# Attention of a hybrid encoder: another place for the softmax division, another rotation, another order of the last half-heads

## The chip, the cores and the metric

One core of a Trainium2 chip runs the whole layer as one program. Its engines are TensorE (PE in the profile: matmuls and transposes), VectorE (DVE), ScalarE (ACT), GpSimd (POOL) and SyncE (SP, which only issues DMAs). Each works through its own instructions in order and waits on semaphores for the others. The time is that of the device, in microseconds, from one launch of the program; the median of several runs counts.

## The reference

One layer of an encoder is applied to two groups of 512 tokens of 1024 channels, in float32. A normalised input goes through one wide projection; its columns feed a recurrent branch (mLSTM) and an attention branch, and two sets of sigmoid gates that merge them. The attention part, and what takes up its result:

```python
qa = (rmsnorm(c_q, g_q) @ w_uq).reshape(B, S, A_HEADS, A_NOPE + A_ROPE)
q_nope = qa[..., :A_NOPE]
q_rope = rope(qa[..., A_NOPE:], cos[:, None, :], sin[:, None, :])
kv = (rmsnorm(c_kv, g_kv) @ w_ukv).reshape(B, S, A_HEADS, A_NOPE + A_V)
k_nope, va = kv[..., :A_NOPE], kv[..., A_NOPE:]
k_rope = rope(k_r, cos, sin)
y_a = mla_attention(q_nope, q_rope, k_nope, k_rope, va) @ w_ao
g_m, g_a = jnp.split(jax.nn.sigmoid(gm), 2, axis=-1)
x = x + (g_m * y_m + g_a * y_a) @ w_out
```

There are 8 heads with 128 plain and 64 rotary channels and 128 value channels. `rope` turns pairs of the 64 rotary channels: with halves x1 and x2 it gives (x1 cos - x2 sin, x1 sin + x2 cos). The attention is a softmax over all 512 tokens. y_m is the recurrent branch's product with w_mo.

## The kernel before

**Tiling.** Activations lie with channels on the 128 partitions and the 512 tokens of a group along the free axis. Every float32 operand of a matmul is split in two parts that the matmul takes: `hi`, a rounding copy made by ACT, and `lo`, the remainder made by DVE (`lo_of`). Each product is three matmuls: hi hi, lo hi, hi lo. So nearly every piece of data costs an ACT cast (0.6 us) and a DVE subtraction (0.7 us).

**Stages around the change.** First the merge gates, 16 pieces taken from the list `bulk` one by one by `merge_gate`, which PE does without waiting; then the first head's projections (`rot_proj`, `proj_hi`, `proj_lo`), the values of all heads (`v_proj`, L723 to L725), the attention loop, and the output products. PE begins the loop at about 640 us and the output products at 861.5.

**The attention loop** runs over 16 half-heads u (8 heads by 2 groups) in 17 rounds, as a pipeline: in round u the scores of u, the last transpose and the weighing of u - 1, and the projections of u + 1. `score` makes 128x512 scores in five matmuls and DVE their maximum (mx), `expo` the exponential with its row sum (ACT: p, den), `turn` and `turn_lo` four transposes (pt) and the split of their result (aph on ACT, apl on DVE), `weigh` the product with the values (av). The division comes after it: DVE takes the reciprocal of the four sums (rc), PE transposes them (`sums_row`), ACT copies them (rb), and two DMAs on POOL's queue write them to memory (rsd) and read them back as one row broadcast over 128 partitions (rb). In `weighed` ACT copies the product from PSUM (oz), POOL multiplies it by rb, and SP's queue writes it to memory (ozd). POOL also makes the remainder of the values (vl).

**Rotation.** `rope_steps` turns the rotary queries of two heads at once: four products with sin over 32 partitions (rs), one with cos, one sum over 128 partitions (rp). `rot_hi` and `rot_lo` then split them into the tiles qs, two casts and two subtractions of 64 partitions per group. This, the weights of later heads (`wa_hi`, `wa_lo`) and the first operands of the output products (`hop_hi` for P1, P2, P6 and P7) are spread over the rounds as filling.

**The output products** (`chain`) multiply by quads of weights in seven block products in place of eight (P1, P2, P7, P6, P5, Q4, P3); one quad is four 512x512 blocks of a weight pair. The operands are sums and differences of blocks: those of the activations are made in `Ops.part` (L913, L919, L920), those of the weights in `Seven.weights` (L972 to L982), on POOL or DVE. First come the four quads of the recurrent branch ("mo", operands hzd), then four of the attention ("ao", operands ozd).

**What sets the order.** In the loop `pinned` is set, and every engine keeps the order in which the code is written. Outside it, and for DMAs, a scheduler orders the instructions of each engine. DMA queues are SP's, ACT's (weights of the quads, `wst`) and POOL's. Tiles are taken from pools of slots; a new tile of a slot waits until its former one has been read.

Of the kernel before, what the change touches and what calls it, by code (L numbers as in the profile page):

```python
# [15 lines left out]
P = 128  # L16
# [46 lines left out]
def encoder_kernel(ctx: ExitStack, tc: tile.TileContext, a):  # L63
# [3 lines left out]
    class Engine:  # L67
# [5 lines left out]
        def __getattr__(self, name):  # L73
# [4 lines left out]
            def call(*args, **kw):  # L78
                r = f(*args, **kw)  # L79
                tc.keep_in_program_order(r)  # L80
                return r
# [619 lines left out]
    Q = Slots("Q", vt=2, rb=1, qkv=12, qst=4, p=3, ph=1, pl=1)  # L701
# [10 lines left out]

    def v_proj(half):
# [3 lines left out]
        for g in range(G):  # L717
            for i in range(NB):
                bk = bank()
# [6 lines left out]
                t = EV(("ch", "bk")[i % 2], "av")  # L726
# [10 lines left out]
    def rope_steps(t, s, nblk):  # L737
        n = 32 * nblk
        for i in range(nblk):
            f, o = slice(32 * i, 32 * i + 32), slice(32 * (i ^ 1), 32 * (i ^ 1) + 32)  # L740
            yield V.tensor_tensor(out=s[o], in0=t[f], in1=sin[f], op=ALU.mult)
        yield V.tensor_tensor(out=t[0:n], in0=t[0:n], in1=cos[0:n], op=ALU.mult)
        yield V.tensor_tensor(out=t[0:n], in0=t[0:n], in1=s[0:n], op=ALU.add)
# [24 lines left out]
    def rot_proj(m, g):  # L768
        t = rots[m, g] = AX("rt", "rp")
        S.copy(t, proj1(was[max(2 * m - 1, 0)], lat["cq"][g], 2, 0, "pj"))  # L770
        rsteps[m, g] = rope_steps(t, AX("rt", "rs"), 4)
# [5 lines left out]
    def rot_hi(m, g):  # L777
        t = rots[m, g]
        qst[m, g] = st = [Q("qst", "qs", F32R) for _ in range(2)]
        for i in range(2):  # L780
            f = slice(64 * i, 64 * i + 64)
            S.copy(st[i][f], t[f])

    def rot_lo(m, g):
        t, st = rots[m, g], qst[m, g]
        for i in range(2):
            f, o = slice(64 * i, 64 * i + 64), slice(64 - 64 * i, 128 - 64 * i)
            V.tensor_tensor(out=st[i][o], in0=t[f], in1=st[i][f].bitcast(F32), op=ALU.subtract)
# [17 lines left out]

    def score(u, i):
        hd, g = halves_[u]
        if i == 0:
# [3 lines left out]
                rc=sm.tile([P, NB], F32, name=nm("rc4"), tag="rc4", bufs=1),  # L813
# [11 lines left out]
    def expo(u, i):  # L825
# [4 lines left out]
        )  # L830

# [35 lines left out]
    def weighed(u):  # L867
# [81 lines left out]
    class Seven:  # L949
# [14 lines left out]
        def weights(self, name):  # L964
# [19 lines left out]
            return wsplit(src)  # L984
# [21 lines left out]
    def chain(quads, head=False, look=4):  # L1006
# [16 lines left out]
        made = {}  # L1023
# [49 lines left out]
    hops = Ops(hraw, None, lambda n: V if n == "P7" else GP)  # L1073
# [13 lines left out]
    def pair(kind, c, ops, put):  # L1087
        e = V if (kind, c) in (("mo", 3), ("ao", 0)) else GP
# [11 lines left out]
    for g in range(G):  # L1100
        rot(0, g, 6)
        rot_hi(0, g)
        rot_lo(0, g)
    kst = []
# [623 lines left out]
```

## Time and profile before

| | |
|---|---|
| median of 3 runs | 1901.38 us (1900.48 to 1904.08) |
| profiled execution, its own time | 1900.27 us |
| span of its instructions | 1898.3 us |
| mean granted TensorE clock | 0.989 |
| PE busy | 1841.2 us (97%) |
| DVE, ACT, POOL busy | 1241.7, 867.5, 420.2 us |

Rows of groups give busy time and the mean of one in ns, then idle time of the engine ahead of them and what ended it. Rows of waits give the waiting instruction and the one that released it, the total, the count and the longest. Rows of the time line give start and duration in us; times in brackets are idle time of the engine ahead of the row. In rows of stages each engine has its busy time in the stretch and its number of instructions; the last three figures are the granted clock of TensorE (1.00 is full speed), the busy share of the DMA engines, and GB/s. A row whose busy time overlaps the next is a pipelined one: matmuls of 0.39 us start every 0.23 us.

### The profile page before, as it was taken

To read this page: it belongs to the slowest core of one execution; us is meant where nothing else is said; L and a number is where in the kernel's file an instruction comes from. 1 tells how busy PE (TensorE), PEld (TensorE's weight loads), DVE (VectorE), ACT (ScalarE), POOL (GpSimd) and SP (SyncE) were. 2 spreads that over 40 slices of the span, in tenths; PEclk is the share of its full clock that TensorE was granted. 3 is DMA by queue.
4 is the path that set the end of the run, shared out by engine and by line. 5 is a ranking of instruction groups with operands and counts; after the bars stand their busy time and mean duration, and the time that the engine had idled before them with its cause. 6 is when DMAs were issued, how large, how long until landed. Compare 5 with 4: busy or idle time off the path is not lost.

```text
span 1898.3 us, 24423 instructions
## 1 busy us (share of the span) xinstructions
PE 1841.2 (97%) x8817; PEld 1526.5 (80%) x8817; DVE 1241.7 (65%) x2081; ACT 867.5 (46%) x1707; POOL 420.2 (22%) x328
## 2 busy tenths in 40 slices
PE   9999999999999999997999999999999999999997
PEld 7889898988887777775878888888888887878786
DVE  6758576766424688865798588445444569878756
ACT  6355556554222666663444356333333344434433
POOL 0100000100000123364031002666465523111000
PEclk9999999999999999998999999999999999999998
DMA  4211211112323423355564342232222347433332
GB/s 167 66 58 49 74 45 68 56 56 78 122 96 102 142 94 96 94 175 197 168 211 153 120 145 83 100 118 105 95 100 97 126 144 236 158 128 100 102 137 94
DMA packets 102024, 216.10 MB, mean 114 GB/s; under 512 B 11536, under 2 KB 22224, under 8 KB 101904
## 3 DMA queue, kind: packets, MB, share of 16 engines
q1 hardware_dynamic: 87456, 165.49, 25.6%
q10 hardware_dynamic: 12096, 43.00, 6.7%
q0 software_dynamic: 2352, 6.07, 1.0%
q8 instruction: 69, 1.13, 0.3%
q14 instruction: 51, 0.42, 0.1%
HBM read 160.24 MB, written 54.26 MB: 113 GB/s over the span
## 4 chain that ended last, share of the span: by engine, by line
PE 45%; DVE 5%; DMA 2%; issue 2%; POOL 1%; ACT 1%; ACTq 0%; SPq 0%; DVEq 0%; POOLq 0%
PE b L1001 12%; PE b L1003 12%; PE b L1002 12%; PE mm L79 2%; PE mm L185 1%; PE mm L184 1%; PE mm L183 1%; DVE xl L154 1%; PE mm L1521 1%; PE mm L1519 1%; PE mm L1520 1%; DVE wp L154 1%; DMA ld<-ozd 1%; POOL oz L79 0%; DMA rb<-rsd 0%
## 5 line engine op out<-in xcount | busy, mean ns | idle before, releaser
L1001 PE MATMUL b<-xh,wp 128*128 128x512 f32 x1148 | 441.7, 393 | 18.7 <-ACT wp L945 13.8
L1002 PE MATMUL b<-xl,wp 128*128 128x512 f32 x1148 | 447.6, 391 | 1.9 <-DVE xl L154 1.9
L1003 PE MATMUL b<-xh,wp 128*128 128x512 f32 x1148 | 444.8, 392 | 1.3 <-DVE wp L154 1.3
L945 ACT CAST wp<-wst 128x512 fp32r<-128x512 f32 (+1 forms) x270 | 164.3, 612 | 308.2 <-PE b L1003 254.4
L154 DVE TENSOR_TENSOR wp<-wst,wp 128x512 fp32r<-128x512 f32 (+1 forms) x270 | 230.2, 855 | 70.6 <-ACT wp L945 70.5
L1001 PEld LDWEIGHTS b<-xh,wp 128*128 128x128 f32 x1148 | 215.9, 188 | 71.7 <-ACT wp L945 17.2
L1002 PEld LDWEIGHTS b<-xl,wp 128*128 128x128 f32 x1148 | 216.0, 188 | 49.7 <-DVE xl L154 3.4
L1003 PEld LDWEIGHTS b<-xh,wp 128*128 128x128 f32 x1148 | 215.7, 188 | 49.4 <-DVE wp L154 2.7
L183 PE MATMUL mm<-hh,whi 128*128 128x512 f32 x560 | 219.5, 392 | 0.0
L184 PE MATMUL mm<-hl,whi 128*128 128x512 f32 x560 | 219.0, 391 | 0.0
L185 PE MATMUL mm<-hh,wlo 128*128 128x512 f32 x560 | 218.8, 391 | 0.0
L1047 DVE TENSOR_TENSOR u<-b,u 128x512 f32<-128x512 f32 x90 | 61.9, 688 | 133.8 <-PE b L1003 84.0
L185 PEld LDWEIGHTS mm<-hh,wlo 128*128 128x128 f32 x560 | 105.5, 188 | 22.2 <-DVE wlo L154 0.3
L184 PEld LDWEIGHTS mm<-hl,whi 128*128 128x128 f32 x560 | 105.6, 189 | 21.6
L183 PEld LDWEIGHTS mm<-hh,whi 128*128 128x128 f32 x560 | 105.6, 188 | 21.5 <-DVE to L382 0.2
L972 POOL TENSOR_TENSOR s<-wst,wst 128x512 f32<-128x512 f32 (+1 forms) x30 | 45.0, 1500 | 320.4 <-DMA wst<-wd 118.1
L168 ACT CAST whi<-wst 128x1024 fp32r<-128x1024 f32 x59 | 62.0, 1051 | 103.5 <-PE mm L184 64.4
L1418 POOL TENSOR_TENSOR sg<-sg,u 128x512 f32<-128x512 f32 x30 | 55.0, 1835 | 204.2 <-DVE u L1047 204.2
L1042 ACT COPY u<-b 128x512 f32<-128x512 f32 x90 | 50.7, 588 | 92.2 <-PE b L1003 66.9
L154 DVE TENSOR_TENSOR xl<-ld,xh 128x512 fp32r<-128x512 f32 x105 | 77.7, 769 | 15.2 <-ACT xh L929 14.6
L154 DVE TENSOR_TENSOR wlo<-wst,whi 128x1024 fp32r<-128x1024 f32 (+2 forms) x61 | 74.2, 1217 | 14.6 <-ACT whi L168 13.4
L79 POOL TENSOR_TENSOR vl<-avt,vh 128x512 fp32r<-128x512 f32 x16 | 20.7, 1291 | 282.3 <-ACT vh L79 282.3
(371 smaller groups left out, 3645.9 us busy)
## 6 DMA issues: line engine op xcount, KB each, us to landing
wst<-w SPq DMA_DIRECT2D x73, 512.0 KB, 3.3
wst<-w ACTq DMA_DIRECT2D x60, 512.0 KB, 3.6
ld<-actd SPq DMA_DIRECT2D x77, 256.0 KB, 2.8
actd<-t SPq DMA_DIRECT2D x40, 256.0 KB, 2.4
x<-x SPq DMA_DIRECT2D x32, 256.0 KB, 4.0
ld<-hzd SPq DMA_DIRECT2D x32, 256.0 KB, 3.5
wst<-wd ACTq DMA_DIRECT2D x16, 512.0 KB, 4.4
actd<-sg SPq DMA_DIRECT2D x30, 256.0 KB, 2.0
```

The costliest lines, as they stand in the source:

```text
L79: r = f(*args, **kw)
L154: e.tensor_tensor(out=out, in0=src, in1=hi.bitcast(F32), op=ALU.subtract)
L168: S.copy(hi[:, :n], st[:, :n])
L183: E.matmul(bk, whi[:, c], hi, start=k == 0, stop=False)
L184: E.matmul(bk, whi[:, c], lo, start=False, stop=False)
L185: last_mm[0] = E.matmul(bk, wlo[:, c], hi, start=False, stop=k == nk - 1)
L945: S.copy(hi, src)
L1001: E.matmul(bk, whi[:, c], hi, start=bool(first) and k == 0, stop=False, **sk)
L1002: E.matmul(bk, whi[:, c], lo, start=False, stop=False, **sk)
L1003: E.matmul(bk, wlo[:, c], hi, start=False, stop=k == self.kh - 1, **sk)
L1047: V.tensor_tensor(out=t, in0=b, in1=t, op=ALU.add if name == "P2" else ALU.subtract)
L1418: e.tensor_tensor(out=sg[at], in0=sg[at], in1=t, op=ALU.mult)
```

## The change

1. *Ahead of the loop*: 10 of the 16 merge gates stay where they were, 6 go between the projections and `v_proj`. The rotation of the shared key is done on 128 partitions and has moved ahead. `v_proj` takes its banks and its output tiles from other pools; the slot `vt` has one buffer in place of two.
2. *Rotation*: the rotary weights' columns are laid out so that the halves of two heads are 64 partitions apart. `rope_steps` needs two products with sin over 64 partitions, one with cos and one sum; the split is one cast and one subtraction over 128 partitions. `rot_put` then copies the 32-partition blocks into the tiles of two heads by eight DMAs on SP's queue.
3. *Division*: for u below 14 (`EVEN`), DVE multiplies the weighed values in PSUM by the broadcast reciprocals, late in the round; ACT's copy and POOL's product are gone. For u = 14 and 15, ACT scales each block of exponentials by its reciprocal ahead of the transposes (`inverse`, `even`), there is no broadcast, and ACT copies the weighed values out. All ozd writes are issued on POOL's queue.
4. *Filling*: the operands of the output products are made in the first and last of four rounds on DVE in place of POOL; the adds of the first mo quad's weights go to DVE. The weights of P1, P2 and P7 of that quad are split in rounds 13 and 14 (`ahead`).
5. *End of the loop*: the last round is written out by itself, with all its transposes behind the weighing of u = 14; `chain` is issued only after the last pinned instruction of DVE, ACT and POOL (`anchors`), with the two first quads already loaded.

```diff
-    Q = Slots("Q", vt=2, rb=1, qkv=12, qst=4, p=3, ph=1, pl=1)
+    Q = Slots("Q", vt=1, rb=1, qkv=12, qst=4, p=4, ph=1, pl=1)
...
-    def rope_steps(t, s, nblk):
-        n = 32 * nblk
-        for i in range(nblk):
-            f, o = slice(32 * i, 32 * i + 32), slice(32 * (i ^ 1), 32 * (i ^ 1) + 32)
+    def rope_steps(t, s):
+        for i in range(2):
+            f, o = slice(64 * i, 64 * i + 64), slice(64 - 64 * i, 128 - 64 * i)
             yield V.tensor_tensor(out=s[o], in0=t[f], in1=sin[f], op=ALU.mult)
...
+    def rot_put(m, g):
+        t, w = rots[m, g]
+        qst[m, g] = [Q("qst", "qs", F32R) for _ in range(2)]
+        for i, st in enumerate(qst[m, g]):
+            for b in range(4):
+                f = 32 * i + 64 * (b // 2)
+                nc.sync.dma_start(st.bitcast(F32)[32 * b : 32 * b + 32], (w, t)[b % 2][f : f + 32])
...
+    def inverse(u, i):
+        x = att[u]
+        V.reciprocal(out=x["rc"][:, i : i + 1], in_=x["den"][:, i : i + 1])
+
+    def even(u, i):
+        x = att[u]
+        S.activation(out=x["p"][i], in_=x["p"][i], func=AF.Copy, scale=x["rc"][:, i : i + 1])
...
         o = EV("ch", "oz")
-        S.copy(o, x["ob"])
-        GP.tensor_tensor(out=o, in0=o, in1=x["rb"], op=ALU.mult)
-        nc.sync.dma_start(ozd[g][hd], o)
+        if u >= EVEN:
+            S.copy(o, x["ob"])
+        else:
+            V.tensor_tensor(out=o, in0=x["ob"], in1=x["rb"], op=ALU.mult)
+        GP.dma_start(ozd[g][hd], o)
...
+        def ahead(self, name):
+            src = self.source(name)
+            t = wpair()
+            hi, lo = t[:, 0 : self.n], t[:, self.n : 2 * self.n]
+            self.w[name] = (hi, lo)
+            return (lambda: S.copy(hi, src)), (lambda: lo_of(lo, src, hi))
...
-    hops = Ops(hraw, None, lambda n: V if n == "P7" else GP)
+    hops = Ops(hraw, None, lambda n: V)
...
-        e = V if (kind, c) in (("mo", 3), ("ao", 0)) else GP
+        e = V if (kind, c) in (("mo", 0), ("mo", 3), ("ao", 0)) else GP
...
+    for _ in range(BULK[1]):
+        merge_gate(*bulk.pop(0))
...
+        if last:
+            score(u, 0)
+            expo(u, 0)
+            score(u, 1)
+            turn(u - 1, 3)
+            turn_lo(u - 1, 3)
+            expo(u, 1)
+            score(u, 2)
+            inverse(u, 0)
+            even(u, 0)
...
+            weigh(u - 1)
+            weighed(u - 1)
+            for i in range(NB - 1):
+                turn(u, i)
+                turn_lo(u, i)
+            continue
...
+    hops.r, hops.t, hops.sums = {}, {}, lambda n: GP
...
+    with ExitStack() as behind:
+        for i in anchors:
+            behind.enter_context(tc.issue_after(i))
+        quads += [pair("ao", c, oops, put_y(c)) for c in range(4)]
+        chain(quads, made=pairs)
...
-BULK = [16]
+BULK = [10, 6]
+EVEN = 14
```

DVE before, at the start of round 3: from the remainder of half-head 2's third block (apl) to half-head 2's reciprocal (rc); the maxima mx are half-head 3's, xl is filling, rs and qs are the rotation.

```order
L79 TENSOR_TENSOR apl_6538<-pt_6580,aph_6537 128x4x128
L79 TENSOR_TENSOR xl_6516<-ld_6201,xh_6515 128x512
L79 TENSOR_TENSOR rs_6458<-rp_6449,sin 32x512
L79 TENSOR_REDUCE mx_6592<-sc_6595 128x1
L79 TENSOR_REDUCE mx_6592<-sc_6608 128x1
L79 TENSOR_TENSOR qs_6602<-rp_6303,qs_6602 64x512
L79 TENSOR_TENSOR qs_6603<-rp_6303,qs_6603 64x512
L79 RECIPROCAL rc_996_6461<-den_6460 128x4
```

The same place of the changed kernel; oz is the division of half-head 1's output, ld a sum of the filling, rp the last step of the rotation.

```order
L79 TENSOR_TENSOR apl_6554<-pt_6597,aph_6553 128x4x128
L79 TENSOR_TENSOR oz_6606<-av_6534,rb_6528 128x512
L79 TENSOR_REDUCE mx_6619<-sc_6622 128x1
L79 TENSOR_TENSOR ld_6215<-ld_6215,ld_6211 128x512
L79 TENSOR_REDUCE mx_6619<-sc_6632 128x1
L79 TENSOR_TENSOR rp_6471<-rp_6471,rs_6472 128x512
L79 RECIPROCAL rc_1001_6483<-den_6482 128x4
```

Five operations stand there in place of six: the division has come in, two splits of the rotation and one product with sin have gone.

POOL before, at the end of the loop: the sums of the output products' operands (ld, L913, L919, L920; wst is a sum of weights) among the reciprocals' DMAs and the last products oz.

```order
L79 TENSOR_TENSOR oz_8205<-oz_8205,rb_8185 128x512
L913 TENSOR_TENSOR ld_8429<-ld_8429,ld_8431 128x512
L975 TENSOR_TENSOR wst_8545<-wst_8545,wst_8547 128x512
L913 TENSOR_TENSOR ld_8438<-ld_8438,ld_8440 128x512
L913 TENSOR_TENSOR ld_8447<-ld_8447,ld_8449 128x512
L913 TENSOR_TENSOR ld_8456<-ld_8456,ld_8458 128x512
L79 TENSOR_TENSOR vl_8297<-avt_8154,vh_8296 128x512
L79 DMA rsd_7_5884<-rb_8302 4x128
L919 TENSOR_TENSOR ld_8505<-ld_8505,ld_8429 128x512
L919 TENSOR_TENSOR ld_8515<-ld_8515,ld_8438 128x512
L919 TENSOR_TENSOR ld_8525<-ld_8525,ld_8447 128x512
L920 TENSOR_TENSOR ld_8505<-ld_8505,ld_8508 128x512
```

POOL now (L946, L952 and L953 are the former L913, L919 and L920; s is a sum of weights).

```order
L79 DMA ozd_6_5491<-oz_8317 128x512
L79 DMA ozd_7_5484<-oz_8396 128x512
L79 DMA ozd_7_5492<-oz_8442 128x512
L946 TENSOR_TENSOR ld_8468<-ld_8468,ld_8470 128x512
L946 TENSOR_TENSOR ld_8477<-ld_8477,ld_8479 128x512
L946 TENSOR_TENSOR ld_8486<-ld_8486,ld_8488 128x512
L946 TENSOR_TENSOR ld_8495<-ld_8495,ld_8497 128x512
L1005 TENSOR_TENSOR s_1556_8690<-wst_8052,wst_8054 128x512
L952 TENSOR_TENSOR ld_8535<-ld_8535,ld_8468 128x512
L952 TENSOR_TENSOR ld_8545<-ld_8545,ld_8477 128x512
L952 TENSOR_TENSOR ld_8555<-ld_8555,ld_8486 128x512
L952 TENSOR_TENSOR ld_8565<-ld_8565,ld_8495 128x512
```

The sums have moved behind the last output's write; five more of them (L1006 and four L953) follow.

ACT now, at the place where the first product of quad 2 gets its weights: xh are casts of POOL's sums, u copies of finished products, wp casts of weights.

```order
L978 CAST wp_8670<-wst_8050 128x512
L991 DMA wst_8729<-w 128x1024
L1085 COPY u_8591<-b_1498_8453 128x512
L978 CAST wp_8693<-s_1556_8690 128x512
L1085 COPY u_8609<-b_1538_8596 128x512
L978 CAST wp_8710<-wst_8048 128x512
L962 CAST xh_8541<-ld_8535 128x512
L991 DMA wst_8731<-w 128x1024
L962 CAST xh_8551<-ld_8545 128x512
L962 CAST xh_8561<-ld_8555 128x512
L1085 COPY u_8642<-b_1498_8453 128x512
L962 CAST xh_8571<-ld_8565 128x512
L978 CAST wp_8751<-wst_8729 128x512
```

The cast for quad 2 (wp_8751) stands behind four casts of sums that POOL makes last (xh_8541 to xh_8571); before, only the DMA of a later weight stood between (wst_8705), and the four casts stood earlier.

More of the change, by code (lines that the diff above doesn't have):

```diff
@@ L1133, in hop_hi, with hop_lo, ahead_hi, ahead_lo @@
         hlo[n] = (lo, src, hi)
+    def hop_lo(n):
+        lo_of(*hlo[n])
     hop_load(0)
+    v_load(0)
+    quads = [pair("mo", c, hops, put_z(c)) for c in range(4)]
+    ahead, anchors = {}, []
+    def ahead_hi(n):
+        hi, ahead[n] = pairs[0].ahead(n)
+        hi()
+    def ahead_lo(n):
+        ahead[n]()
     pinned[0] = True
     for u in range(NU + 1):
-        now, then, nxt = u < NU, u > 0, u + 1 < NU
+        now, then, nxt, last = u < NU, u > 0, u + 1 < NU, u == NU - 1
         m, r = u // 4, u % 4
@@ L1140, in encoder_kernel, with fill, p7_sum @@
         more = m < 3
-        def at(row, *alts):
-            return row == r and all(alts)
-        sub = None
-        if at(3, now):
-            hops.sums = lambda n: V if n == "P7" or m == 3 else GP
-            sub = hops.part("P6", m)
+        todo_ = {}
+        def fill(slot):
+            for f, *args in todo_.get(slot, ()):
+                f(*args)
+        if now and r == 0:
+            p7 = [None]
+            def p7_sum():
+                p7[0] = hops.part("P7", m)
+            todo_ = {
+                "a": [(p7_sum,)],
+                "mid": [(hop_hi, "P1", hops.part("P1", m)), (hop_hi, "P2", hops.part("P2", m))],
+                "d": [(hop_lo, "P1")],
+                "e": [(hop_lo, "P2")],
+                "late": [(lambda: hop_hi("P7", p7[0]),)],
+                "f": [(hop_lo, "P7")],
+            }
+            if more:
+                todo_["mid"].insert(0, (wa_hi, 2 * m + 1, RO))
+                todo_["d"].insert(0, (wa_lo, 2 * m + 1, RO))
+                todo_["end"] = [(rot_proj, m + 1, 0)]
+                if m == 0:
+                    todo_["late"].append((wa_hi, 1, QK))
+                    todo_["f"].append((wa_lo, 1, QK))
@@ new lines, in encoder_kernel, with p6_sum, p6_lo @@
+        if (more and r == 3) or (m == 3 and r == 1):
+            p6 = [None]
+            def p6_sum():
+                p6[0] = hops.part("P6", m)
+            def p6_lo():
+                hop_lo("P6")
+                if m < 3:
+                    hop_load(m + 1)
+            todo_ = {"a": [(p6_sum,)], "mid": [(lambda: hop_hi("P6", p6[0]),)], "d": [(p6_lo,)]}
+            if more:
+                todo_["b"] = [(rot_lo, m + 1, 1)]
+                todo_["late"] = [(wa_hi, 2 * m + 3, QK)]
+                todo_["f"] = [(wa_lo, 2 * m + 3, QK)]
+                todo_["end"] = [(rot_put, m + 1, 1)]
@@ L1179, in encoder_kernel @@
         if then:
[L1180 removed]
+            if u - 1 < EVEN:
+                V.reciprocal(out=att[u - 1]["rc"], in_=att[u - 1]["den"])
             turn_lo(u - 1, 3)
[L1182 to L1187 removed]
+        odd(u, 0)
+        fill("c")
         if nxt:
@@ L1259, in encoder_kernel @@
             WX = Slots("WX", "right", wst=2, s3=2, wp=1)
+            pairs = {i: quads[i][1]() for i in range(2)}
         if u == NU - 2:
```

229 lines of the change are left out of this document (104 added, 125 removed).

## The prediction

> **What bounds the kernel now.** I read the page's busy table, then the list of what TensorE waited for around the change, then busy time and clock by stage.
>
> ```profile
> PE 1841.2 (97%) x8817; PEld 1526.5 (80%) x8817; DVE 1241.7 (65%) x2081; ACT 867.5 (46%) x1707; POOL 420.2 (22%) x328
> PE b L1001 <- ACT wp L945: 11.4, 1, 11.4
> PE pt L79 <- DVE rc L79: 10.9, 9, 2.4
> PE mm L723 <- DVE ql L154: 2.9, 1, 2.9
> 653.00:840.00 187.00, 176.67 (x866) 140.10 (x865) 150.76 (x228) 123.03 (x275) 64.19 (x64) 0.99 0.32 98
> 840.00:862.00 22.00, 17.74 (x72) 13.09 (x71) 14.03 (x18) 8.79 (x21) 18.57 (x17) 0.84 0.63 223
> 862.00:900.00 38.00, 26.57 (x110) 21.42 (x109) 17.92 (x27) 13.28 (x26) 11.96 (x7) 0.87 0.62 214
> ```
>
> TensorE (PE) is busy 97% of the 1898.3 us span, and its matmuls stay what they are but for two transposes. So only PE's idle time, 57 us in all, and what runs at a lowered clock behind it can be won. Where the change reorders work, PE waits three times: 2.9 us ahead of the value projections, 10.9 us in nine pieces for the reciprocals of the softmax sums, 11.4 us at the boundary to the output products. Idle time is followed by a slow clock at some places and not at others (the last three figures are granted clock, DMA share and GB/s):
>
> ```profile
> 613.00:620.00 7.00, 6.41 (x19) 4.46 (x20) 6.40 (x11) 3.89 (x7) 0.00 (x0) 0.76 0.22 73
> 682.00:689.00 7.00, 6.69 (x27) 5.45 (x28) 4.46 (x7) 2.71 (x7) 2.35 (x3) 0.76 0.21 65
> 739.00:746.00 7.00, 7.00 (x36) 5.80 (x37) 5.79 (x8) 4.17 (x11) 2.37 (x3) 1.00 0.20 62
> 894.00:899.00 5.00, 4.03 (x11) 3.18 (x12) 3.69 (x6) 2.14 (x4) 0.00 (x0) 0.58 1.02 385
> ```
>
> Seven us at 0.76 lose 7 x 0.24 = 1.7 us; five at 0.58 lose 2.1 us. At 739 PE had paused about as long as at 682 and lost nothing. [...]
>
> **Ahead of attention.** Six merge gates now stand between the projections and the value projections: 288 matmuls at the 0.23 us of the rows at 861 (quoted below), 65 us of cover for the VectorE work that PE waited for. Gone are 2.9 us and the 1.7 of slow clock. I leave 0.7 for a wait between the two groups of value projections, which now share other buffers: **-3.9** (bounds -4.6, and 0 if the wait only moves).
>
> **The reciprocals.** In every half-head PE transposes the reciprocals, and waits when VectorE (DVE) reaches them late. Two places, DVE's rows and then PE's:
>
> ```profile
> 676.27 0.68 DVE L79 TENSOR_TENSOR apl<-pt,aph 128x512 fp32r<-128x512 f32 x1
> 676.87 0.68 DVE L79 TENSOR_TENSOR xl<-ld,xh 128x512 fp32r<-128x512 f32 x1
> 677.58 1.66 DVE L79 TENSOR_TENSOR rs<-rp,sin 32x512 f32<-32x512 f32 x1
> 679.26 1.29 DVE L79 TENSOR_REDUCE mx<-sc 128x1 f32<-128x512 f32 x2
> 680.58 1.39 DVE L79 TENSOR_TENSOR qs<-rp,qs 64x512 fp32r<-64x512 f32 x2
> 681.98 0.18 DVE L79 RECIPROCAL rc<-den 128x4 f32<-128x4 f32 x1
> 682.31 0.27 PE L79 MATMUL pt<-ident,rc 128*4 128x128 f32 x1 [2.42 <-DVE rc L79]
> 693.45 0.68 DVE L79 TENSOR_TENSOR wlo<-wst,whi 128x512 fp32r<-128x512 f32 x1
> 694.05 1.32 DVE L79 TENSOR_REDUCE mx<-sc 128x1 f32<-128x512 f32 x2
> 695.28 0.68 DVE L79 TENSOR_TENSOR rp<-rp,cos 128x512 f32<-128x512 f32 x1
> 695.88 0.69 DVE L79 TENSOR_TENSOR xl<-ld,xh 128x512 fp32r<-128x512 f32 x1
> 696.49 0.17 DVE L79 RECIPROCAL rc<-den 128x4 f32<-128x4 f32 x1
> 696.80 0.27 PE L79 MATMUL pt<-ident,rc 128*4 128x128 f32 x1 [0.33 <-DVE rc L79]
> ```
>
> From the end of apl (the remainder of the third block of softmax weights) to the reciprocal DVE works 5.1 us at the first place (676.87 to 681.98: six operations) and 3.0 us at the second (693.45 to 696.49: five). PE would have taken the result 5.1 - 2.4 = 2.7 us after that stretch began, and 3.0 - 0.3 = 2.7 at the second place: one constant. So the wait is the DVE work in that stretch less 2.7 us. In the new order the stretch holds, as the rows of the new order in the section on the change show for round 3, the division from PSUM, two maxima and up to two other operations: five in rounds 3, 4, 7, 8, 11, 12 and 13, at 0.6 each from start to start 3.1 us, a wait of 0.4; in the others less, or six behind a rotary projection that gives PE 1.4 us (six matmuls) more: none. The division reads PSUM like apl, whose 0.68 I take for it; bounds 0.6 to 1.7 (rs above, which stood against GpSimd). By this 7 x 0.4 = 2.8 us are left of 10.9 - 1.8 = 9.1 (the ninth piece, 1.8 us, is in the tail below): -6.3, and -1.7 of slow clock at 682. ScalarE (ACT) has a cast more in line in rounds 4, 8, 12 and 13: +0.5 in all. **-7.5** (bounds -8.5 and +1).
>
> The rest lies under PE outside these stretches. DVE had 150.8 of 187 us; 14 divisions at 0.68 add 9.5, five rotary operations per group in place of eight take away 18 at 0.6 or more, 11 us, and the sums that come over from GpSimd are a few at 0.68. If that cover failed, it would show as reciprocal waits, priced below. The rotated queries now go by eight small copies per group on SP's queue, 48 in the loop, with the value loads behind them, which have about half a half-head (7 us) to land.
>
> **The tail.** In the last two half-heads the division is done on ACT before the transposes.
>
> ```profile
> 845.13 0.27 PE L79 MATMUL pt<-ident,rc 128*4 128x128 f32 x1 [1.82 <-DVE rc L79]
> L79 ACT ACTIVATE p<-sc,mx 128x512 f32<-128x512 f32 x59 | 40.9, 693 | 24.1 <-DVE mx L79 24.0
> ```
>
> Two transposes (0.5) and the wait of 1.8 go; eight scalings come, of about 0.7 each by the exponential's 693 ns, the last of which stands between the last exponential and its transpose, with a reciprocal: 0.9 to 1.9, and the other three of that half-head partly. I put this at **0** (bounds -3 and +3).
>
> **The boundary.** Here is the chain of waits that led to PE's 11.43 us:
>
> ```profile
> 861.51 0.40 PE L1001 MATMUL b<-xh,wp 128*128 128x512 f32 x1
> 861.75 0.39 PE L1002 MATMUL b<-xl,wp 128*128 128x512 f32 x1
> 872.94 6.36 POOL oz L79
> 879.32 2.00 DMA ozd<-oz
> 881.82 5.50 DMA ld<-ozd
> 887.38 6.41 DMA ld<-ozd
> 893.87 0.33 ACTq L958
> 894.97 0.80 PE L1001 MATMUL b<-xh,wp 128*128 128x512 f32 x1 [11.43 <-ACT wp L945]
> ```
>
> GpSimd's (POOL) last product oz waits for the broadcast reciprocals and then runs 6.36 us; its write to memory (ozd) is next, SP's queue stands behind that, so its loads start late, and ACT's DMA for quad 2's weights goes only as the second of these lands. None of this is left: the last two half-heads' outputs are only copied by ACT, nothing waits for a broadcast there, and the ozd writes have left SP's queue for POOL's. 11.4 us and 2.1 of slow clock go.
>
> What is late next: the sums of the recurrent branch's halves. Before they ran beside the tail (POOL is busy 18.6 of the 22 us from 840 on); now they stand behind the last half-head on POOL, and ACT's casts of them stand ahead of its cast for quad 2's first product. PE starts the products at 861.5 and has eight before that one, 96 matmuls at 0.23: 22 us of cover. POOL needs 14 operations:
>
> ```profile
> L919 POOL TENSOR_TENSOR ld<-ld,ld 128x512 f32<-128x512 f32 x4 | 5.0, 1267 | 0.0
> 857.65 6.18 DVE L79 TENSOR_TENSOR xl<-ld,xh 128x512 fp32r<-128x512 f32 x1
> 872.64 1.89 DVE L154 TENSOR_TENSOR xl<-ld,xh 128x512 fp32r<-128x512 f32 x3
> 875.05 2.49 DVE L154 TENSOR_TENSOR xl<-ld,xh 128x512 fp32r<-128x512 f32 x4
> ```
>
> 14 x 1.27 = 17.8 us, from 1.5 us after PE's start (ACT's copy and two DMA issues come first), and two casts of 0.6: 20.5 us, so undisturbed they are just in time and PE waits 0. But DVE and POOL hold each other up: a DVE xl of 0.6 took 6.18 us under back-to-back sums at 857, and POOL's oz of 1.28 took 6.36 while DVE ran eight operations from 872.6 on. In the new stretch DVE has some 14 operations with two SBUF inputs, each waiting for a cast, so that they come singly. If each costs POOL half a microsecond (its own 0.6, not always in full), 7 us are added: 27.5 - 22 = 5.5 us of wait, and 1.6 of slow clock. If POOL's sums shut DVE out in a body, two spells of 6 us fall on the remainders that PE needs: 12, and 2.1. I take the alternating case: -13.5 + 7.1 = **-6.4** (bounds -13.5 and +0.6).
>
> [...]
>
> **Sum.** -3.9 - 7.5 + 0 - 6.4 = -17.8 us, from the profiled execution's own 1900.27: 1882.5. The runs' median is 1.1 above that execution, so I forecast **1883**.
>
> **Rivals.**
> - *The sums shut DVE out* (boundary +0.6 in place of -6.4): 1883 + 7 = **1890**. For it: the 6.18. Against: at 872 it was DVE that kept POOL out, and there it had the longer run of operations ready.
> - *No wait at the boundary*: 1883 - 7 = **1876**. For it: the 20.5 against 22. Against: it leaves 1.5 us for all contention.
> - *The reciprocal waits stay*, since the division was put into the very stretch that decides them: if one operation in the stretch doubles as rs did (1.66), each of 14 half-heads waits 1 us more or so, and the clock drops at one place or two: 7.5 + 1 less gain, **1891**. Against: the division has its input in PSUM, as apl has, whose 55 instances stay at 0.68.
> - *DVE waits for the broadcast.* The division now heads DVE's queue five operations before the reciprocal; behind it stand the maxima for which the exponentials and so PE's next transposes wait. The reciprocals' way through memory is POOL's:
>
> ```profile
> L79 POOL DMA_DIRECT2D rsd<-rb x15: 560/560/668, 656.1 to 852.2; - x15
> DMA to landing us min/median/max: 2.5/3.4/4.9
> ```
>
> From reciprocal to landing: 0.3 to PE, 0.3 transposes, 0.3 copy on ACT, 0.56 issue, 2.7 landing, 0.57, 3.4: 8.1 us. The next reciprocal comes 14.5 us after this one (681.98, 696.49), the division 3.1 before it: 11.4, so 3 us of margin, 1.5 with the longest landing. The outputs' writes of 256 KB now go on the same queue. If they hold the small ones up, DVE waits what exceeds 3 us, in 14 half-heads. To lose the whole gain and 3.8 us more it must be 21.6 / 14 = 1.5 us each, a landing 4.5 us later than now: **1905** or more. For it: a write takes 2.0 us (879.32) and nothing of that size was on this queue but the broadcast. Against: the write is issued after the broadcast has landed, and half a half-head ahead of the next small one.
>
> [...]
>
> **Chances.** Forecast 0.42; sums shut DVE out 0.16; no wait at the boundary 0.14; reciprocal waits stay 0.10; DVE waits for the broadcast 0.11; several of these costs at once, ending near the old time, 0.07. A measurement of this kernel tells about 0.2% (3.8 us) from no change. Faster: 0.42 + 0.16 + 0.14 + 0.08 of the fourth = 0.80; same: 0.07 + 0.02 = 0.09; slower: 0.11. The range runs from 1872 (no wait at the boundary, the tail 3 better, nothing left ahead of attention) to 1897 (sums shut DVE out, the tail 3 worse, half the reciprocal waits back) and leaves out the broadcast rival; the forecast's own is 1878 to 1888.
>
> **What would show it.** Right: no PE wait at the value projections; reciprocal waits of 3 us in all, in rounds 3, 4, 7, 8, 11, 12 and 13; no chain through ozd at the boundary, but one from POOL's sums over ACT's cast to the first product of quad 2, with 3 to 8 us of idle time; DVE's division near 0.68 us. Wrong: idle time of DVE ahead of the division (fifth case), of PE on value loads (SP's queue), or a division of 1 us and more. The stages behind 900 us keep their order on every engine, so they should last the same to 1 us; more would mean that something carries over.

## The result, and the profile after

The changed kernel takes 1883.89 us (median of 4 runs, 1881.14 to 1890.15), the one before 1902.73 us in the same rounds (1900.48 to 1905.74): a ratio of 0.9905 with a 95% interval of 0.9875 to 0.9934, some 19 us less. The profiled execution has a span of 1883.4 us. The forecast was 1883. That the total fits is luck: two terms of the sum missed, by about as much in opposite directions, as a table by stage shows. Its bounds are the same matmuls in both programs (their start times in the two traces).

| stage | before | changed | difference | forecast |
|---|---|---|---|---|
| matmul 2800 (at 499 us) to the first score | 140.99 | 137.65 | -3.3 | -3.9 |
| first score to the scores of half-head 14 | 188.93 | 181.59 | -7.3 | -7.5 |
| from there to the first output product | 33.77 | 34.64 | +0.9 | 0 |
| first to 192nd matmul of the output products | 57.03 | 56.21 | -0.8 | -6.4 |
| 192nd to 576th matmul | 92.82 | 93.47 | +0.6 | 0 |
| the rest | 886.96 | 880.49 | -6.5 | 0 |

What lies ahead of matmul 2800 is 1.6 us longer in this trace; over the kernels that follow it varies by 3.4 us, with the same instructions. With it the two traces lie 14.9 us apart, where the medians lie 19 apart: the changed kernel's traced execution took 1885.22 us, more than its median, and that of the kernel before 1900.27, less than its own. In the traced executions of two experiments (e7 and e9) the matmuls of the output products took 843 and 828 ns on average in place of 390 (spans of 5577 and 4728 us), with a recorded granted clock of 1.00. So PE's times cannot be read from these two, and what slowed PE there (throttling, says the expectation of e9) is not shown.

What TensorE (PE) waited for between 590 and 900 us, now (waiting instruction, releaser, us, times, longest):

```profile
PE b L1046 <- DVE wp L155: 10.9, 1, 10.9
PE pt L79 <- DVE rc L79: 4.3, 11, 1.0
PE pt L79 <- DVE apl L79: 3.0, 1, 3.0
PE mm L725 <- ACT wvh L159: 1.7, 1, 1.7
PE pt L79 <- ACT p L79: 1.4, 2, 0.7
PE av L79 <- ACT aph L79: 0.9, 2, 0.7
```

The waits for reciprocals went from 10.9 to 4.3 us, but at the boundary there is a wait of 10.9 us where there was one of 11.4. It is another wait. Here are VectorE (DVE), GpSimd (POOL) and PE in the time line at that place:

```profile
854.62 18.86 DVE L155 TENSOR_TENSOR wp<-wst,wp 128x512 fp32r<-128x512 f32 x2 [3.78 <-ACT wp L978]
855.03 5.04 POOL L946 TENSOR_TENSOR ld<-ld,ld 128x512 f32<-128x512 f32 x4
860.04 1.28 POOL L1005 TENSOR_TENSOR s<-wst,wst 128x512 f32<-128x512 f32 x1
861.29 4.93 POOL L952 TENSOR_TENSOR ld<-ld,ld 128x512 f32<-128x512 f32 x4
866.19 1.25 POOL L1006 TENSOR_TENSOR wst<-wst 128x512 f32<-128x512 f32 x1
867.41 4.91 POOL L953 TENSOR_TENSOR ld<-ld,ld 128x512 f32<-128x512 f32 x4
872.93 0.80 PE L1046 MATMUL b<-xh,wp 128*128 128x512 f32 x1 [10.87 <-DVE wp L155]
```

POOL's 14 sums follow each other from 855.03 to 872.3 without a gap, 17.3 us. In DVE's row two subtractions are merged. The first, the remainder of the weights for P6, the fourth product, has 0.7 us of work and lasts 18.26 us, to 872.87, half a microsecond after POOL has ended. The second, for the product behind it, takes 0.68. PE has only P1, P2 and P7 and two matmuls of P6 ahead of its wait, from 853.3 to 862.1.

In the loop, this is round 3 again, from the end of apl at 676.1:

```profile
676.12 0.68 DVE L79 TENSOR_TENSOR oz<-av,rb 128x512 f32<-128x512 f32 x1
676.72 0.68 DVE L79 TENSOR_REDUCE mx<-sc 128x1 f32<-128x512 f32 x1
677.31 0.68 DVE L79 TENSOR_TENSOR ld<-ld,ld 128x512 f32<-128x512 f32 x1
677.91 0.68 DVE L79 TENSOR_REDUCE mx<-sc 128x1 f32<-128x512 f32 x1
678.51 0.68 DVE L79 TENSOR_TENSOR rp<-rp,rs 128x512 fp32r<-128x512 f32 x1
679.11 0.17 DVE L79 RECIPROCAL rc<-den 128x4 f32<-128x4 f32 x1
679.43 0.27 PE L79 MATMUL pt<-ident,rc 128*4 128x128 f32 x1 [0.28 <-DVE rc L79]
```

Five operations, 3.0 us, no operation over 0.69: a wait of 0.28 where it was 2.42.

### The profile page after: what moved, and what is told of

Read it like the earlier page. It is cut to its first block, busy times and chain, and to the rows that moved or that the text cites. A ratio compares the mean times of both kernels' runs of the same rounds, so it can differ in the third digit from the quotient of the medians.

```text
span 1883.4 us, 24476 instructions
## 1 busy us (share of the span) xinstructions
PE 1831.4 (97%) x8815; PEld 1525.6 (81%) x8815; DVE 1238.8 (66%) x2084; ACT 860.7 (46%) x1690; POOL 393.3 (21%) x316
## 4 chain that ended last, share of the span: by engine, by line
PE 47%; DVE 7%; issue 1%; ACT 1%; DMA 0%; ACTq 0%; DVEq 0%; POOLq 0%
PE b L1044 12%; PE b L1046 12%; PE b L1045 12%; PE mm L79 2%; DVE wp L155 2%; DVE xl L155 1%; PE mm L186 1%; PE mm L184 1%; PE mm L185 1%; PE mm L1606 1%; PE mm L1607 1%; PE mm L1608 1%; ACT p L79 0%; DVE x L1543 0%; DVE t L943 0%
## 5 line engine op out<-in xcount | busy, mean ns | idle before, releaser
L155 DVE TENSOR_TENSOR wp<-wst,wp 128x512 fp32r<-128x512 f32 (+1 forms) x268 | 248.1, 928 | 68.9 <-ACT wp L978 68.7
L383 DVE TENSOR_TENSOR tg<-rs,mm 128x512 f32<-128x512 f32 x32 | 22.0, 686 | 82.8 <-PE mm L186 77.6
```

The source lines that it names most:

```text
L155: e.tensor_tensor(out=out, in0=src, in1=hi.bitcast(F32), op=ALU.subtract)
```

## The experiments

Each experiment changes the changed kernel by the diff shown and was timed in five rounds beside the kernel before on the same chip. Stage lengths are those of the table above; the changed kernel has 137.65, 181.6, 34.6, 56.2.

### e1: the changed kernel again

> The changed kernel itself, on the chip and in the rounds in which the next three run. Both theories: about 19 us less than the kernel before (1883 against 1902), with the 10.9 us wait of PE at the fourth product (P6, quad 0) again, and one VectorE weight remainder (wp) that lasts 18 to 19 us for two operations.

1884.75 us against 1904.53 (ratio 0.990, 0.9885 to 0.9915), a PE wait of 10.84 us at the same matmul, and stages of 137.65, 181.52, 34.34 and 56.30 us. The stages up to the 576th matmul repeat to 0.3 us, so they tell apart what the whole times do not. The tail repeats less well across kernels: it is 32.8 us in e8 and 33.6 in e2, whose edits do not touch it.

### e2: the boundary's sums on VectorE

```diff
-    hops.r, hops.t, hops.sums = {}, {}, lambda n: GP
+    hops.r, hops.t, hops.sums = {}, {}, lambda n: V
```

> The sums for P5 and Q4 (12 operations) at the boundary on VectorE in place of GpSimd, nothing else. Theory A (GpSimd's gapless run of 14 sums shuts out VectorE's weight remainder): GpSimd's run is 3 operations, no wp operation lasts over 3 us, and PE's wait at P6 falls from 10.9 to about 1 to 3 us, since VectorE now makes 12 sums at 0.6 (7 us) within the 8.2 us of cover that P1, P2 and P7 give; no slow clock after it. 8 to 11 us faster than the changed kernel. Theory B (the remainder waits for its cast, its weights or a buffer, and the sums only run at the same time): the wait stays or grows by the 7 us of added VectorE work; 0 to 7 us slower. Theory C (the operands for Q4 come late anyway): the wait moves to Q4 or to quad 2 and stays 8 us or more; no difference.

1878.37 us, ratio 0.9861 (0.9846 to 0.9875). PE's waits at the boundary are now these two:

```profile
PE b L1044 <- ACT wp L978: 1.5, 1, 1.5
PE b L1046 <- DVE wp L155: 1.0, 1, 1.0
```

The stage is 48.5 us, 7.7 shorter, though DVE has 7 us more to do in it. Behind the 1.5 us the clock was halved again (the stretch of 1.49 us in the last section). By the ratios the kernel is 7 to 8 us faster than the changed one, where 8 to 11 were expected. This is theory A; B and C would have kept the wait.

### e3: only the sums for Q4 on VectorE

```diff
-    hops.r, hops.t, hops.sums = {}, {}, lambda n: GP
+    hops.r, hops.t, hops.sums = {}, {}, lambda n: V if n == "Q4" else GP
```

> Only the 8 sums for Q4 on VectorE, the 4 for P5 left on GpSimd. Theory A: GpSimd's gapless run is 4 sums and 2 or 3 weight sums, 8 to 9 us from its start in place of 17.3, so the held remainder ends 8 to 9 us earlier than in the changed kernel and PE's wait falls from 10.9 to 2 to 3 us; 8 to 10 us faster than the changed kernel. Theory B: wait unchanged. Theory C: the wait moves to Q4 or quad 2.

1880.12 us, ratio 0.9877 (0.9861 to 0.9894): by the ratios 4 to 5 us less than the changed kernel, where 8 to 10 were expected. DVE, POOL and PE:

```profile
852.02 8.95 DVE L155 TENSOR_TENSOR wp<-wst,wp 128x512 fp32r<-128x512 f32 x2 [3.70 <-ACT wp L978]
852.44 5.04 POOL L946 TENSOR_TENSOR ld<-ld,ld 128x512 f32<-128x512 f32 x4
857.45 1.27 POOL L1005 TENSOR_TENSOR s<-wst,wst 128x512 f32<-128x512 f32 x1
869.34 0.50 PE L1046 MATMUL b<-xh,wp 128*128 128x512 f32 x1 [4.28 <-DVE wp L155]
```

Fewer sums, a shorter hold: the first of the two merged subtractions, P6's, lasts 7.25 us in place of 18.26 and ends at 859.27, again half a microsecond after the end of POOL's run (five sums, to 858.72). PE does not wait for it at all. The wait of 4.3 us is another one, two products later: it is for P5's remainder (868.61 to 869.29), which stands behind sums that DVE now makes. The stage is 49.9 us. So in these two traces the length of DVE's operation went with that of POOL's run: 18.26 us with 17.3, 7.25 with 6.3.

### e4: output products not held behind the loop

```diff
-        for i in anchors:
+        for i in anchors[:0]:
```

> The output products are no longer held behind the last instruction of the loop; GpSimd's sums run beside the last two half-heads. Theory A: most of GpSimd's run is over when the weight remainder comes, PE's wait at the boundary falls to 0 to 4 us, but VectorE's remainders of those sums and ACT's casts get into the tail: tail 0 to 6 us longer; in all 3 to 10 us faster than the changed kernel. Theory B: the boundary wait stays near 11 us.

1884.61 us, ratio 0.9898 (0.9883 to 0.9913): no difference. The boundary stage is 43.9 us with no wait, 12.3 shorter, but the tail is 49.9 us, 15.3 longer: the hold has moved there.

```profile
839.18 11.26 DVE L1015 TENSOR_TENSOR wst<-wst 128x512 f32<-128x512 f32 x1
852.30 2.07 PE L79 MATMUL av<-apl,vh 128*128 128x512 f32 x4 [8.31 <-DVE apl L79]
```

With nothing held back, a weight sum of the output products also got into DVE's queue ahead of the softmax remainders, was shut out for 11.26 us, and PE waited for what stood behind it. The hold again ended half a microsecond after POOL's run (849.89). Theory A had the boundary right, but gave the tail 0 to 6 us more.

### e5: the division behind the reciprocal

```diff
+        if 1 < u < NU:
+            weighed(u - 2)
...
             odd(u, 3)
-            if then:
-                weighed(u - 1)
```

(`weighed(u - 2)` stands just behind `turn_lo(u - 1, 3)`, and in the last round behind `even(u, 1)`.)

> VectorE's division (oz) is moved from five operations ahead of the next reciprocal to just behind it; nothing else. Theory D (PE's wait for the reciprocal is VectorE's work in that stretch less 2.7 us): the stretch is 0.6 us shorter in every round, the reciprocal waits fall from 4 us in 11 pieces to at most 0.7, and the loop is 3 us shorter. Theory E (the waits come from something else, such as the maxima or the accumulator read): waits unchanged, or moved to the weighing, which now waits for the division: 0 to 5 us longer.

1892.47 us, ratio 0.9953 (0.9939 to 0.9966), where the changed kernel had 0.990 to 0.9905: 9 to 10 us slower, and the loop is 191.64 us, 10 longer.

```profile
PE av L79 <- DVE oz L79: 12.2, 13, 1.6
PE pt L79 <- DVE rc L79: 1.4, 3, 0.8
```

The reciprocal waits fell in the sense of theory D, from 4.3 to 1.4 us (at most 0.7 was expected). But there is one bank for the weighed values: the next weighing now waits for the division, 13 times. A term that theory D left out decided. Theory E had named it, at 0 to 5 us. The division's place ahead of the reciprocal is the cheaper one.

### e6: the division on GpSimd again

```diff
-            V.tensor_tensor(out=o, in0=x["ob"], in1=x["rb"], op=ALU.mult)
+            S.copy(o, x["ob"])
+            GP.tensor_tensor(out=o, in0=o, in1=x["rb"], op=ALU.mult)
```

> The division of the first 14 half-heads again as before the change: copy from PSUM on ScalarE, product on GpSimd; all else as changed. Theory F (the division on VectorE does not by itself win the loop; the shorter rotation and the order do): reciprocal waits fall from 4 to about 1 us as in the late division, rotation steps rise to 0.8 or more beside GpSimd's products: loop from 2 us shorter to 1 longer. Theory G (taking GpSimd's products out of VectorE's way is what won): the reciprocal waits come back to 8 to 11 us and the loop is 4 to 8 us longer.

1883.98 us, ratio 0.9904 (0.9889 to 0.9919): the same as the changed kernel; the loop is 182.16 us, 0.6 longer. So moving the division to DVE is worth next to nothing by itself. Round 3, DVE and POOL:

```profile
674.85 1.59 DVE L79 TENSOR_TENSOR ld<-ld,ld 128x512 f32<-128x512 f32 x1
674.62 1.28 POOL L79 TENSOR_TENSOR oz<-oz,rb 128x512 f32<-128x512 f32 x1 [5.03 <-ACT oz L79]
PE pt L79 <- DVE rc L79: 4.1, 10, 0.8
```

DVE has one operation less in the stretch, but the sum beside POOL's product takes 1.59 us in place of 0.68: what is saved is lost to the hold. Theory F has the size; that the waits would fall to 1 us it had wrong.

### e7 and e9: the weights of P6 and of quad 1's P1 ahead of the sums

```diff
         else:
+            for q, n in ((0, "P6"), (1, "P1")):
+                hi, lo = pairs[q].ahead(n)
+                hi()
+                lo()
             weighed(u - 1)
```

> The remainders of the weights of P6 (quad 0) and P1 (quad 1) are made before the last half-head's output copy, so before GpSimd's sums begin; GpSimd's run of 14 stays. Theory A (lock): the next VectorE operation with two inputs from SBUF is held to the end of the same run instead, but PE has five products of cover in place of three, 5.5 us more: wait 10.8 to 5 us, 5 to 6 us faster than the changed kernel. Theory B (late cast, weights or buffer of that one remainder): no wait of more than 2 us is left, 9 us or more faster.

> The kernel of e7 once more, since e7's profiled execution had TensorE throttled throughout (span 5577 us) and shows nothing of the boundary; its other six executions had a median of 1883.96. Theory A (lock): the wait is less than 10.8 but not gone, 3 to 6 us, at the next remainder with two SBUF inputs, which ends with GpSimd's run of sums. Theory B: no wait over 2 us at the boundary.

Medians of 1884.29 and 1882.61 us, ratios 0.9908 (0.9893 to 0.9924) and 0.9884 (0.9869 to 0.9899): by the ratios between 1 us more and 4 us less than the changed kernel, where 5 to 6 less were expected. PE's wait cannot be read from these traces. What DVE and POOL did can; this is e9:

```profile
2129.93 17.07 DVE L155 TENSOR_TENSOR xl<-ld,xh 128x512 fp32r<-128x512 f32 x1 [7.09 <-ACT xh L962]
2127.96 4.96 POOL L946 TENSOR_TENSOR ld<-ld,ld 128x512 f32<-128x512 f32 x4
2145.19 1.26 POOL L1008 TENSOR_TENSOR wst<-wst,wst 128x512 f32<-128x512 f32 x1
```

The two remainders were done ahead, in 0.7 us each, and the next operation with two inputs from SBUF, an operand's remainder, was held 17.07 us, to the end of POOL's run. So the hold did not belong to that one remainder, its cast or its buffer: here it fell on the operation that came next. Why the time fell by less than the cover of two more products stays open.

### e8: the merge gates back

```diff
-BULK = [10, 6]
+BULK = [16, 0]
```

> All 16 merge gates ahead of the projections again, none between these and the value projections. If they were the cover: PE's wait ahead of the first value projection is back, 1 to 3 us (the rotation there is four VectorE products in place of eight, so less than the 2.9 of before is possible), with 1.7 us of slow clock if it is over 2.4; the 1.7 between the two groups stays: 1 to 4.5 us slower than the changed kernel. If the shorter rotation had already removed the wait: no difference within 0.5 us in the trace.

1884.37 us, ratio 0.9909 (0.9892 to 0.9925). The first stage is 136.45 us: 1.2 shorter than with the gates as cover, and PE waits for

```profile
PE mm L725 <- ACT wvh L159: 1.7, 1, 1.7
```

alone. Neither expectation had this. The gates were not what took the wait of 2.9 us away; between the projections they even cost a wait of 0.9 us at their start.

### e10: the rotation in pieces of 32 partitions

```diff
         for i in range(2):
-            f, o = slice(64 * i, 64 * i + 64), slice(64 - 64 * i, 128 - 64 * i)
-            yield V.tensor_tensor(out=s[o], in0=t[f], in1=sin[f], op=ALU.mult)
+            for j in range(2):
+                b = 64 * i + 32 * j
+                f, o = slice(b, b + 32), slice((b + 64) % 128, (b + 64) % 128 + 32)
+                q = V.tensor_tensor(out=s[o], in0=t[f], in1=sin[f], op=ALU.mult)
+            yield q
```

> Each product with sin is made in two pieces of 32 partitions in place of one of 64 (12 more VectorE operations in the loop), in the same layout and at the same places; all else as changed. Theory D (reciprocal wait = VectorE's work in the stretch less what PE has to do): two operations come into the stretch in rounds 1, 5 and 9, one in rounds 2, 6 and 10: 3 x 1.2 + 3 x 0.6 = 5.4 us more of reciprocal waits (4.3 to 9.7), the loop 5.4 us longer, with a slow clock or two up to 8. Rival (VectorE, idle for 20% of the loop, takes 12 operations of 0.6 without PE noticing): 0 to 1 us.

1893.61 us, ratio 0.9947 (0.9934 to 0.9961): 8 to 10 us slower than the changed kernel. The loop is 189.56 us, 8.0 longer, the first stage 139.87, 2.2 longer.

```profile
PE pt L79 <- DVE rc L79: 10.9, 14, 2.2
PE mm L184 <- DVE ql L155: 3.1, 1, 3.1
```

The reciprocal waits are 10.9 us where the work in the stretch gave 9.7, and behind the projections, at the first of the gates, PE waits 3.1 us. Twelve operations of 0.6 us in the loop, and no more, undo the loop's whole gain and two thirds of that ahead of it.

### e11: four edits together

```diff
         if u >= EVEN:
-            S.copy(o, x["ob"])
+            V.tensor_copy(out=o, in_=x["ob"])
...
     def even(u, i):
         x = att[u]
+        if u == NU - 1 and i > 1:
+            V.tensor_scalar(out=x["p"][i], in0=x["p"][i], scalar1=x["rc"][:, i : i + 1], scalar2=None, op0=ALU.mult)
+            return
```

(with the edits of e2, e7 and e8)

> Four edits on the changed kernel: the boundary's sums on VectorE (e2), P6's and quad 1's P1 remainders ahead of them (e7), all merge gates ahead again (e8), and in the last half-head the scaling of blocks 2 and 3 and the two output copies on VectorE in place of ScalarE. The edits act at four places: boundary wait 10.9 to at most 1 us and its slow clock gone (-11 to -12 of the trace's stretch from the first output product to the 192nd matmul, where e2 had -7.7); ahead of attention -1.2; ScalarE is 1.3 + 1.2 us earlier in the last half-head, so PE's 3.0 us wait there falls to 0 to 1.5 and the tail is 2 to 4 us shorter, its slow clock (1.7) perhaps with it. In all 12 to 17 us faster than the changed kernel, 8 to 10 faster than e2.

1866.92 us, ratio 0.9811 (0.9798 to 0.9825): 36 us less than the kernel before, the fastest of all. Stages: 136.45, 181.52, 30.59, 45.31. So -1.2, 0, -4.0 and -10.9, each within its range or at its edge, and -3.1 more up to the 576th matmul. Between 520 and 900 us PE waits, among others, for

```profile
PE pt L79 <- DVE rc L79: 3.3, 10, 0.8
PE pt L79 <- DVE apl L79: 2.1, 1, 2.1
PE b L1047 <- ACT u L1088: 1.5, 1, 1.5
```

The wait for apl, in the last half-head, was expected at 0 to 1.5 us.

### e12: the outputs' writes on SP's queue

```diff
-        GP.dma_start(ozd[g][hd], o)
+        nc.sync.dma_start(ozd[g][hd], o)
```

> The outputs' writes (ozd) on SP's queue as before the change, in place of GpSimd's; all else as changed. Theory H (those writes are off every path in the loop; GpSimd's other DMAs are issued in about 0.55 us either way): loop within 0.5 us, reciprocal waits 4 us, landing of the small writes and of the broadcast unchanged (median 3.3 and shorter); at the boundary the wait of 10.9 us is the same, since GpSimd's sums still start behind the loop: 0 to 1 us different. Rival (the writes hold up the broadcasts on the shared queue, as round 14's wait of 1 us for the broadcast suggests): that wait goes and landings shorten, loop 1 us or more shorter. Second rival (SP's queue, standing behind a write that waits for the division, loads values late): PE or ScalarE waits on value loads, loop 2 us or more longer.

1869.30 us, ratio 0.9826 (0.9804 to 0.9849): one line, and some 15 us less than the changed kernel (10.5 of them in the tail and at the boundary together, 3.1 up to the 576th matmul). All three theories missed it. The loop is the same (181.44), the tail 36.7 us, 2.1 longer, the boundary 43.7 us, 12.5 shorter, without the wait at P6. On POOL:

```profile
837.41 1.29 POOL L946 TENSOR_TENSOR ld<-ld,ld 128x512 f32<-128x512 f32 x1
838.66 2.53 POOL L952 TENSOR_TENSOR ld<-ld,ld 128x512 f32<-128x512 f32 x2
846.51 2.97 POOL L953 TENSOR_TENSOR ld<-ld,ld 128x512 f32<-128x512 f32 x2
PE pt L79 <- DVE apl L79: 3.4, 1, 3.4
PE sc L79 <- DVE ql L79: 1.5, 1, 1.5
```

The output products are held behind the last instruction of the loop on each engine. On POOL that was the write of the last output, which waits for the last weighing (its issue is at 854.5 in the changed kernel, just ahead of the sums). Without the writes it is the values' remainder of half-head 14, and the sums start as their operands land, run beside the tail and are over at 849.5, before PE begins the products. DVE's operations of the output products are still held back, unlike in e4, so little stands in the way of the softmax remainders.

## Why the prediction was right, and where it was wrong

**Bound and place**: right for the stages that were reordered. There idle time of PE and the clock behind it are what moved, and the three waits named were the large ones that changed. Two smaller ones grew that were not foreseen: between the two groups of value projections (0.5 to 1.7 us, 0.7 had been left for it) and for apl in the last half-head (none to 3.0). What moved behind 1000 us (the rest, below) is not idle time.

**Ahead of attention** (-3.9, measured -3.3): the size was right, the cause wrong. I put it to the six gates as cover. With the gates back (e8) the wait stays away. With eight more VectorE products in the rotation of queries and key there (e10), PE waits 3.1 us at the first gate, where it waits 0.9 now. So the shorter rotation is what e10 points to; a kernel with the gates back and the long rotation, which would settle it, was not run.

**The reciprocals** (-7.5, measured -7.3): right, in rule and size. The rule (DVE's work in the stretch less 2.7 us) gave 0.4 in rounds 3, 4, 7 and so on; the trace shows 0.26 to 0.29 in all seven. It foretold the direction in e5 and, within 1.2 us, the 10.9 of e10. What it missed are rounds 5 and 9 (0.30 each), round 1 (0.83), and round 14 (0.96), where DVE's division waited for the broadcast: the rival in which the division heads the queue, in one round of 14. e1 has 0.40 there and e12 still 0.89, so sharing the queue with the writes was not its cause. The division took 671 to 691 ns in 14 instances, as forecast. But none of them ran beside a sum of POOL, so they do not show that POOL cannot hold it. The one that did is in e4: 0.67 us at 837.23, beside a sum from 836.82 to 838.10, where a sum of DVE beside POOL's product took 1.59 us in e6. Others with an input from PSUM did so in the trace of before: 10 remainders apl, 19 maxima and 24 operations on finished products (u) began inside a TENSOR_TENSOR of POOL and took 672 to 693 ns, where 90 remainders of weights (wp, both inputs in SBUF) took 683 to 1801.

**The tail** (0, measured +0.9): within its bounds. PE waits 3.0 us there for apl, ScalarE being late. e11 takes four instructions off ScalarE and has a tail 4.0 us shorter, but only 0.9 of it is this wait (2.1). The mean granted clock of the stage is 1.00 there and 0.90 now, which is 3.5 us of 34.6, and e8, which leaves the tail alone, has 0.95 and is 1.9 us shorter.

**The boundary** (-6.4, measured -0.8): here the prediction failed, at the step "I take the alternating case". The rival "the sums shut DVE out", to which I gave 0.16, is what happened, and in full: 18.26 us for one operation of 0.7. e2, e3 and e9 show it from three sides: without POOL's run no hold (no remainder of weights there over 1.8 us), with a shorter run a shorter one (7.25), with those remainders done early the next is held (17.07). Its 1890 is about what would have been measured without the 6.5 us of the rest (below). I also had the place wrong: I followed ACT's queue to quad 2, with eight products of cover, and did not ask which remainder DVE would be at when the run begins. That was P6's, with three. The old chain through ozd did go, as foreseen. And I booked the writes' move from SP's to POOL's queue as a gain alone; e12 shows that the move itself made the sums late, because POOL's sums were held behind the last write.

The hold went beyond one instruction: DVE got in at none of 13 ends of POOL's instructions while the next was ready. So did the 6.18 us of before: they cover four whole sums of POOL. Nor did the earlier start decide: DVE's row begins at 854.62, POOL's first sum at 855.03 (it issued a DMA from 854.47 on). But it is not always so. At a dozen other places of the same trace, DVE got in after one instruction, and POOL's next, though it followed without a gap, was the one held:

```profile
1197.22 1.69 DVE L155 TENSOR_TENSOR wp<-wst,wp 128x512 fp32r<-128x512 f32 x1 [1.26 <-ACT wp L978]
1197.07 1.29 POOL L1006 TENSOR_TENSOR wst<-wst 128x512 f32<-128x512 f32 x1
1198.32 1.74 POOL L1505 TENSOR_TENSOR sg<-sg,u 128x512 f32<-128x512 f32 x1
```

So both of the ends that the prediction weighed occur, and what decides between them stays open. The writes on POOL's queue cost the loop nothing that the traces show: POOL's issues there took 530 to 674 ns with them, 560 to 668 before, and the loop is as long in e12 (181.44 us in place of 181.59).

**The rest** (0, measured -6.5): not foreseen, and it makes up for the boundary. Without it the forecast would have been some 6 us too low. It is no wait. Nearly all of it (643.5 to 637.7 us) lies in the products between 1147 and 1790 us. In the stretch from 1200 us on, before and now:

```profile
L1002 PE MATMUL b<-xl,wp 128*128 128x512 f32 x848 | 331.1, 391 | 0.9 <-DVE xl L154 0.9
L1045 PE MATMUL b<-xl,wp 128*128 128x512 f32 x835 | 324.7, 389 | 0.8 <-DVE xl L155 0.8
```

The matmuls start every 228.5 ns on average before and every 226.9 now (of those less than 300 ns apart), with the same order on each engine. The average hides that only a part of them differs: of 2740 starts between 1147 and 1790 us before, 868 come 228 ns or more behind the one ahead, in rows of up to 17, and the others after 224 to 227. Now it is 91 of 2746, and in the experiments (e7 and e9 aside) 94 to 118. Between 500 and 640 us, ahead of all that the change reorders in the loop, both kernels start one every 226.9 ns. The other kernels' rest is between 879.9 and 883.9 us, all below 886.96, and the medians on one chip (e1) are 19.8 us apart where the stages that the change reorders sum to 10. So it seems to belong to the kernel. There is only one trace of the kernel before; what causes it was not tried. The change also lists the PSUM banks in another order, but only those of the products from 853 us on; those between 1147 and 1790 us are listed alike in both kernels. So that order does not explain this part. That tiles lie elsewhere is a candidate that is left.

## What to carry to other kernels

Where GpSimd has a run of operations ready without a gap, price the case in which a VectorE operation with two inputs from SBUF that meets it lasts to the end of the run (it did in the changed kernel and in e3, e4 and e9, for 18.26, 7.25, 11.26 and 17.07 us, and did not at a dozen places of one trace), and ask first which one that is and how much cover the engine behind it has; here splitting the run (e3), starting it earlier (e12) and giving the sums to VectorE (e2) took 4 to 5, some 15 and 7 to 8 us off the time. When a DMA issue moves to another engine, ask what stands behind it there and which data it waits for: here POOL's sums stood behind the last write and began at 855.03, where with the writes on SP's queue they were over at 849.5, and that cost 10 us at the place and 15 in all. Where a serial chain runs through one engine, compare its work between two fixed points with that of the waiting engine: that difference foretold the waits to some tenths of a microsecond in most rounds.

## What the runs showed of the hardware that was not expected

Besides the hold over many instructions (18.26 us) and the two spacings of the matmul starts, the clock: PE paused twice at the beginning of the attention's output products, for 1.06 and 0.84 us before and for 1.27 and 0.84 us now. Behind the ones the clock held, behind the others it fell. The traces show what differs. In the traces of before and now the granted clock changes only at points that lie whole multiples of 3.41 us apart (before: 614.91, 618.32, 683.17, 686.59 and so on), and it is 1.00 or 0.50 between two of them. Here are such stretches, six of the kernel before, then two of now. The first figure is the length, the second PE's busy time, so that the difference is its idle time; the last three are clock, DMA share and GB/s:

```profile
679.76:683.17 3.41, 0.99 (x6) 0.76 (x6) 3.35 (x7) 3.12 (x9) 0.73 (x2) 1.00 0.41 130
683.17:686.59 3.42, 3.42 (x10) 2.65 (x9) 2.36 (x3) 0.45 (x1) 1.67 (x2) 0.50 0.26 77
734.37:737.79 3.42, 2.17 (x12) 1.47 (x10) 3.36 (x4) 1.28 (x4) 2.66 (x2) 1.00 0.20 77
737.79:741.20 3.41, 2.23 (x11) 1.88 (x12) 3.35 (x6) 2.50 (x7) 1.48 (x2) 1.00 0.24 77
963.07:966.48 3.41, 2.35 (x11) 1.46 (x9) 3.41 (x7) 1.14 (x2) 0.00 (x0) 1.00 0.81 221
966.48:969.90 3.42, 2.58 (x11) 1.99 (x11) 3.42 (x7) 1.74 (x3) 2.29 (x1) 1.00 0.83 280
954.67:958.08 3.41, 1.50 (x6) 0.60 (x4) 3.41 (x6) 1.32 (x3) 0.00 (x0) 1.00 0.88 251
958.08:961.50 3.42, 3.22 (x8) 2.55 (x9) 3.42 (x7) 1.33 (x3) 3.13 (x1) 0.50 0.89 275
```

The pause of 2.42 us at 682 lay in one stretch, and the next ran at half the clock. The equally long one at 739, which the prediction could not explain, was cut in two, 1.24 and 1.18, and cost nothing. In the output products the two pauses fell into two stretches before, and now for the most part into one (1.91 us). Between 560 and 1000 us of these two traces, all 8 stretches at full clock with 1.82 us or more of idle time were followed by a halved one, and none of the 237 with 1.69 us or less. In all twelve traces with a clock it was all 31 with 1.79 us or more, and of the 1472 with 1.71 us or less, one (1.49 us, in e2). So the pause at 682 cost 1.7 us more (half of the 3.42 us behind it) and the one at 739 nothing, by where they fell, and a difference of that size between two of these kernels can be chance.

In e4, e11 and e12 the stage from the 192nd to the 576th matmul was 3 us shorter: PE paused 1.0 us less in it, and no stretch was halved.
